# Half-group loads of x and a longer look-ahead in an RMSNorm and matmul kernel

## The chip, the cores and the metric

One core of a Trainium2 chip runs the kernel. The metric is the device time of one execution in microseconds (us). The time of a kernel is the median of repeated runs; a profile comes from one further execution, whose own time stands beside it. In the profile, PE is TensorE (PEld its weight loads), ACT is ScalarE, DVE is VectorE, POOL is GpSimd, and SP is the engine that issues nearly all transfers. Transfers run on 16 DMA engines.

## The reference

Every row of x is divided by its root mean square, scaled by gamma, and multiplied by a weight matrix. x has 16 x 1024 rows of 512 floats (33.6 MB), the output has 768 floats for each row (50.3 MB).

```python
batch, seq, dim, out_dim = 16, 1024, 512, 768
rms = np.sqrt(np.mean(x ** 2, axis=-1, keepdims=True) + eps)
x_norm = x / rms * gamma
return np.matmul(x_norm, weight).astype(np.float32)
```

## The kernel before

The 16,384 rows are cut into 128 tiles of 128 rows, and eight tiles make a group (G = 8), so there are 16 groups. A group of x is one SBUF tile `xt` of 128 partitions x 8 x 512 floats; each partition holds eight rows that lie one after the other in memory, so a whole group is one stretch of 16 KB for each partition, and a group of the output one of 24 KB. Groups 2 to 13 are loaded and stored whole, with one transfer each (2 MB in, 3 MB out). The first two and the last two groups are cut into smaller parts by the table `parts` (line 45): 1, 2, 1, 2, 2 tiles, then 4, 4, and at the end 4, 4 and 2, 2, 2, 1, 1. For a tile i, `first[i]` and `size[i]` are the part that it lies in, and `rows` (line 54) is that part's piece of x or of the output.

Per tile: POOL casts x to bf16 for a pair of tiles (`cast`, line 86, into `xb`), ACT squares it with a running sum (line 90, `jk`), takes the root (line 94), and DVE the reciprocal (line 96). PE transposes the bf16 words (line 113, into PSUM `tp`), DVE copies them to SBUF (line 120, `xT`), and PE multiplies with the weights in four steps of 512 and 256 columns (line 147, PSUM `ops`). ACT finishes the even tiles and DVE the odd ones: they scale the product with the reciprocal into the output tile `ot` (lines 130 and 132). `store` (line 144) sends a part when its last tile is done.

The order of all instructions is written by hand. In the main loop, pair j computes tiles 2j and 2j+1; at its head it issues the loads that `load_until(2*j + AHEAD)` finds due, then the cast of pair j+3 and the norms of pair j+1, and among its matmuls the transposes of a later pair. `load_until` (with `load`, line 75, doing the transfer) walks through the list `starts` and issues each load whose first tile lies below the given bound. Before the loop, three tiles are loaded, then the weights in two halves, then all that starts below AHEAD.

Loads and stores are issued by SP in program order: an instruction that waits holds up all behind it. Each transfer signals one of eight semaphores in rotation, and waits at its issue for the transfer that had the same semaphore before. There are 5 buffers for groups of x, 4 for cast pairs, 3 for groups of the output.

Of the kernel before, what the change touches and what calls it, by code (L numbers as in the profile page):

```python
# [18 lines left out]
def kernel(  # L19
# [8 lines left out]
    nc = tc.nc  # L28
    P = 128

    x = x.flatten_outer_dims()
    out = out.flatten_outer_dims()
# [3 lines left out]
    NT = N // P  # L36
    NP = NT // 2
    G = 8
    NG = NT // G
    AHEAD = 20  # L40
    WIDE = 512

    parts = {0: [1, 2, 1, 2, 2], 1: [4, 4], NG - 2: [4, 4], NG - 1: [2, 2, 2, 1, 1]}
    first, size = {}, {}
    for g in range(NG):
        i = g * G
# [4 lines left out]

    def rows(ap, i):
        return ap[first[i] * P:(first[i] + size[i]) * P, :].rearrange("(p t) d -> p t d", t=size[i])

    singles = ctx.enter_context(tc.tile_pool(name="singles", bufs=1))
    xin = ctx.enter_context(tc.tile_pool(name="xin", bufs=5))
# [8 lines left out]
    x_tiles, xb_tiles, tp_tiles, rstd_of, xT_tiles, o_tiles = {}, {}, {}, {}, {}, {}  # L67

    def held(tiles, i, n=1):
        return tiles[i // G][:, i % G:i % G + n, :]  # L70

    def load(i):
        if i // G not in x_tiles:
            x_tiles[i // G] = xin.tile([P, G, D], F32, name="xt")
        nc.sync.dma_start(out=held(x_tiles, i, size[i]), in_=rows(x, i))

    starts = [i for i in range(NT) if first[i] == i]

    def load_until(i):
        while starts and starts[0] < i:  # L80
            load(starts.pop(0))
# [52 lines left out]
    def accumulator():  # L134
        return opsum.tile([P, 2, WIDE], F32, name="ops").rearrange("p a b -> p (a b)")

# [5 lines left out]
    def store(i):  # L142
        if i == first[i] + size[i] - 1:
            nc.sync.dma_start(out=rows(out, i), in_=held(o_tiles, first[i], size[i]))

    def matmul(i, k, acc, lo, hi):
        nc.tensor.matmul(out=acc[:, lo:hi], lhsT=xT_tiles[i // 2][:, i % 2, k // 2, :, k % 2], rhs=w_bf[:, k, lo:hi],  # L147
                         start=(k == 0), stop=(k == K - 1))


    def matmuls(i, acc, ks, feed=None):
        for k in ks:
            matmul(i, k, acc, 0, WIDE)
            if feed:
                feed()
            matmul(i, k, acc, WIDE, O)

# [19 lines left out]
    with tc.manual_schedule():  # L177
# [9 lines left out]
        for h in range(2):  # L187
            nc.sync.dma_start(out=w_f32[:, 2 * h:2 * h + 2, :].rearrange("p c o -> p (c o)"), in_=wv[:, h, :])
        load_until(AHEAD)


        warm = singles.tile([P, WIDE], BF16)
        nc.vector.memset(warm, 0.0)  # L193
# [6 lines left out]
        def warm_up(n):  # L200
            for _ in range(n):
                nc.tensor.matmul(out=spare[:, :WIDE], lhsT=warm[:, :P], rhs=warm, start=True, stop=True)  # L202

        w_bf = singles.tile([P, K, O], BF16)

        def weights(k, engine, lo=0, hi=O):
            scale(engine, w_bf[:, k, lo:hi], w_f32[:, k, lo:hi], g_sb[:, k % 2, k // 2:k // 2 + 1])
# [21 lines left out]
        acc = [accumulator() for _ in range(4)]  # L229
        weights(0, nc.vector, 0, WIDE)  # L230
        weights(0, nc.vector, WIDE, O)
# [26 lines left out]
        for j in range(2, NP):  # L258
            load_until(2 * j + AHEAD)
            if j + 3 < NP:  # L260
# [61 lines left out]
```

## Time and profile before

| | us |
|---|---|
| median of 10 runs | 211.41 |
| lowest and highest of them | 211.07, 211.89 |
| the profiled execution | 211.58 |
| its span, first to last instruction | 209.8 |
| PE busy | 201.2 |
| ACT busy | 158.2 |
| DVE busy | 111.8 |
| POOL busy | 66.2 |

The span is what the profile covers; 1.8 us of the profiled execution's time lie around it. A busy time is the sum of an engine's instructions. Transfers have two times of their own: that of their issue on SP, and that from issue to landing, when the last of the 16 DMA engines has signalled. Typical ones of before, in us from issue to landing: 16.0 for a whole group's store (3 MB), 20.5 for a whole group's load (2 MB), 13.8 for a load of 1 MB, 8.9 for a store of 384 KB. The core reads 35.13 MB and writes 50.33 MB, 407 GB/s over the span.

### The profile page before, as it was taken

The numbers are of one execution on the slowest core, as the hardware profiler recorded it, in microseconds if no ns is written. First come the engines' busy times: TensorE is split into PE (matmuls) and PEld (weight loads), VectorE is DVE, ScalarE is ACT, GpSimd is POOL, SyncE is SP. The second block draws the span as 40 slices with busy tenths as digits, with TensorE's granted clock in tenths as the row PEclk, the third lists the DMA queues.
The fourth block names the chain that finished last, engine by engine and source line by source line (L and its number), as shares of the span: only waits on it lengthen the run. The fifth ranks groups of instructions, "written<-read, shape, count | busy, mean of one in ns | idle before, by whom it ended". The sixth has DMA issues, their size and how long they took to land.

```text
span 209.8 us, 3598 instructions
## 1 busy us (share of the span) xinstructions
PE 201.2 (96%) x1297; PEld 138.0 (66%) x1297; DVE 111.8 (53%) x204; ACT 158.2 (75%) x388; POOL 66.2 (32%) x71
## 2 busy tenths in 40 slices
PE   7999999999999999999999999999999999999960
PEld 2566777666776666776667766667766677666630
DVE  2555654564465456545644654565456446545630
ACT  4589787788778777877887787778778877877830
POOL 2057341607233323323252332324133305050000
PEclk9999999999999999999999999999999999999997
DMA  6999999999999999999999999999999999998983
GB/s 219 412 429 412 390 419 410 429 421 440 444 406 451 414 434 426 423 434 422 440 423 437 417 442 431 415 440 409 444 414 447 405 426 391 424 432 357 412 349 148
DMA packets 8070, 85.69 MB, mean 408 GB/s; under 512 B 1138, under 2 KB 1140, under 8 KB 3956
## 3 DMA queue, kind: packets, MB, share of 16 engines
q1 hardware_dynamic: 7776, 85.46, 97.1%
q8 instruction: 10, 0.16, 0.3%
q10 hardware_dynamic: 276, 0.00, 0.1%
q14 instruction: 8, 0.07, 0.1%
HBM read 35.13 MB, written 50.33 MB: 407 GB/s over the span
## 4 chain that ended last, share of the span: by engine, by line
PE 94%; DVE 1%; ACT 1%; issue 0%
PE ops L147 78%; PE tp L113 13%; PE ops L202 3%; DVE ot L132 1%; ACT ot L130 0%; DVE xT L120 0%; ACT jk L90 0%; PE tp L224 0%; ACT rms L94 0%; DVE warm L193 0%; DVE rstd L96 0%; DVE eps_sb L195 0%
## 5 line engine op out<-in xcount | busy, mean ns | idle before, releaser
L147 PE MATMUL ops<-w_bf,xT 128*128 128x256 bf16 (+1 forms) x1024 | 194.0, 326 | 0.1
L147 PEld LDWEIGHTS <-xT 128*128 128x128 bf16 x1024 | 100.2, 98 | 56.2 <-DVE xT L120 0.9
L86 POOL CAST xb<-xt 128x1024 bf16<-128x1024 f32 (+1 forms) x65 | 65.5, 1016 | 120.6 <-DMA xt<-in_x_dram 66.1
L120 DVE COPY xT<-tp 128x1024 bf16<-128x1024 bf16 (+1 forms) x67 | 44.5, 667 | 81.3 <-PE tp L113 81.3
L130 ACT ACTIVATE ot<-ops,rstd 128x768 f32<-128x768 f32 (+1 forms) x65 | 58.1, 894 | 37.7 <-PE ops L147 36.9
L90 ACT ACTIVATE jk<-xt 128x512 bf16<-128x512 f32 x128 | 78.7, 619 | 1.1 <-DMA xt<-in_x_dram 1.1
L113 PE MATMUL tp<-ident_f,xb 128*128 128x128 f32 x256 | 69.1, 275 | 0.1
L132 DVE TENSOR_SCALAR ot<-ops,rstd 128x768 f32<-128x768 f32 (+1 forms) x65 | 64.5, 992 | 2.9 <-PE ops L147 2.8
L113 PEld LDWEIGHTS tp<-ident_f,xb 128*128 128x128 f32 x256 | 36.0, 142 | 4.8 <-issue 1.0
L90 ACT ACTIVATION_READ_ACCUMULATOR jk<-xt 128x1 f32 x128 | 24.4, 190 | 0.0
L94 ACT ACTIVATE rms<-ssq,eps_sb 128x2 f32<-128x2 f32 (+1 forms) x64 | 18.9, 295 | 2.0
L96 DVE RECIPROCAL rstd<-rms 128x2 f32<-128x2 f32 (+1 forms) x64 | 10.0, 156 | 3.3 <-ACT rms L94 3.2
L202 PE MATMUL ops<-warm 128*128 128x512 bf16 x15 | 5.7, 531 | 1.2 <-DVE eps_sb L195 1.2
L202 PEld LDWEIGHTS <-warm 128*128 128x128 bf16 x15 | 1.7, 124 | 3.1 <-issue 1.4
L130 ACT ACTIVATE w_bf<-w_f,g_sb 128x768 bf16<-128x768 f32 x2 | 1.9, 935 | 2.4 <-DMA w_f<-in_weight_dram 2.4
L184 ACT ACT_TABLE_LOAD x1 | 1.3, 1283 | 1.8 <-issue 1.8
L86 DVE CAST xb<-xt 128x512 bf16<-128x512 f32 x2 | 1.1, 557 | 2.3 <-DMA xt<-in_x_dram 2.3
L132 DVE TENSOR_SCALAR w_bf<-w_f,g_sb 128x512 bf16<-128x512 f32 (+2 forms) x3 | 1.4, 485 | 0.9 <-DMA w_f<-in_weight_dram 0.9
L193 DVE MEMSET warm<- 128x256 uint32 x1 | 0.3, 272 | 0.9 <-PEq L303 0.9
L224 PE MATMUL tp<-ident_f,g_row 2*128 2x2 f32 x2 | 0.4, 264 | 0.3 <-DVE xT L120 0.3
L224 PEld LDWEIGHTS tp<-ident_f,g_row 2*128 2x128 f32 x2 | 0.3, 201 | 0.5 <-DVE xT L120 0.5
masks.py:199 POOL TENSOR_SCALAR_AFFINE_SELECT ident_f<-ident_f 128x128 f32<-128x128 f32 x1 | 0.3, 294 | 0.1
(7 smaller groups left out, 0.8 us busy)
## 6 DMA issues: line engine op xcount, KB each, us to landing
out_dram<-ot SPq DMA_DIRECT2D x12, 3072.0 KB, 16.0
xt<-in_x_dram SPq DMA_DIRECT2D x12, 2048.0 KB, 20.5
out_dram<-ot SPq DMA_DIRECT2D x4, 1536.0 KB, 11.5
out_dram<-ot SPq DMA_DIRECT2D x6, 768.0 KB, 9.1
xt<-in_x_dram SPq DMA_DIRECT2D x4, 1024.0 KB, 13.8
xt<-in_x_dram SPq DMA_DIRECT2D x6, 512.0 KB, 14.3
w_f<-in_weight_dram SPq DMA_DIRECT2D x2, 768.0 KB, 6.9
out_dram<-ot SPq DMA_DIRECT2D x4, 384.0 KB, 8.9
```

Of the source, the lines that this page charges most:

```text
L86: engine.tensor_copy(out=xb_tiles[i // 2][:, i % 2:i % 2 + n, :], in_=held(x_tiles, i, n))
L90: nc.scalar.activation(out=jk, in_=held(x_tiles, i)[:, 0, :], func=AF.Square, accum_out=ssq)
L94: nc.scalar.activation(out=rms[:, :n], in_=ssq[:, :n], func=AF.Sqrt, scale=1.0 / D, bias=eps_sb)
L96: nc.vector.reciprocal(out=rstd[:, :n], in_=rms[:, :n])
L113: nc.tensor.transpose(out=tp_tiles[j][:, t, h, :], in_=words[:, lo:lo + P], identity=ident_f)
L120: nc.vector.tensor_copy(out=dst[:, t:t + n, :], in_=src[:, t:t + n, :])
L130: nc.scalar.mul(out=dst, in_=src, mul=r)
L132: nc.vector.tensor_single_scalar(out=dst, in_=src, scalar=r, op=mybir.AluOpType.mult)
L147: nc.tensor.matmul(out=acc[:, lo:hi], lhsT=xT_tiles[i // 2][:, i % 2, k // 2, :, k % 2], rhs=w_bf[:, k, lo:hi], start=(k == 0), stop=(k == ...
L184: nc.scalar.preload_act_table(AF.Sqrt)
L202: nc.tensor.matmul(out=spare[:, :WIDE], lhsT=warm[:, :P], rhs=warm, start=True, stop=True)
L224: nc.tensor.transpose(out=gp[:, c, :], in_=g_row[:, :, c], identity=ident_f[:2, :2])
```

## The change

The look-ahead goes from 20 to 24 tiles, and no load has more than four tiles: a whole group comes in two loads, each of 8 KB for each partition, from the same rows of memory as before (so a partition's two pieces of 8 KB lie one behind the other, and the pieces of one load have a pitch of 16 KB). Both halves still go into one SBUF tile `xt`. Parts of four tiles and fewer are loaded as before, apart from the look-ahead. The stores are not touched.

```diff
-    AHEAD = 20
+    AHEAD = 24
...
+    HALF = 4
...
     def load(i):
         if i // G not in x_tiles:
             x_tiles[i // G] = xin.tile([P, G, D], F32, name="xt")
-        nc.sync.dma_start(out=held(x_tiles, i, size[i]), in_=rows(x, i))
-
-    starts = [i for i in range(NT) if first[i] == i]
+        n = min(size[i], HALF)
+        t = i - first[i]
+        nc.sync.dma_start(out=held(x_tiles, i, n), in_=rows(x, i)[:, t:t + n, :])
+
+    starts = [i for i in range(NT) if (i - first[i]) % HALF == 0]
```

## The prediction

> **What bounds the kernel now.** I read the page's busy rows first, then its queue row, then the busy time by stretches, the timeline of the SP queue, SP's waits, and the time from issue to landing of single transfers.
>
> ```profile
> PE 201.2 (96%) x1297; PEld 138.0 (66%) x1297; DVE 111.8 (53%) x204; ACT 158.2 (75%) x388; POOL 66.2 (32%) x71
> PE   7999999999999999999999999999999999999960
> DMA  6999999999999999999999999999999999998983
> q1 hardware_dynamic: 7776, 85.46, 97.1%
> ```
>
> Two resources are full at once: TensorE, and the 16 DMA engines, all fed through SP's one queue. By stretches (after the engines' columns: granted clock, DMA share, GB/s):
>
> ```profile
> 72.00:84.00 12.00, 12.00 (x81) 8.40 (x79) 6.75 (x12) 9.52 (x25) 4.17 (x4) 1.00 1.01 431
> 132.00:144.00 12.00, 12.00 (x81) 8.39 (x80) 6.61 (x13) 9.64 (x24) 4.17 (x4) 1.00 1.00 427
> 205.00:206.00 1.00, 0.00 (x0) 0.00 (x0) 0.00 (x0) 0.00 (x0) 0.00 (x0) 1.00 1.00 402
> 206.00:207.00 1.00, 0.00 (x0) 0.00 (x0) 0.00 (x0) 0.00 (x0) 0.00 (x0) 1.00 0.32 126
> 207.00:208.00 1.00, 0.00 (x0) 0.00 (x0) 0.00 (x0) 0.00 (x0) 0.00 (x0) 0.80 0.14 55
> 208.00:209.00 1.00, 0.00 (x0) 0.00 (x0) 0.00 (x0) 0.00 (x0) 0.00 (x0) 0.50 0.03 12
> ```
>
> In the middle PE has no idle time. Its work by the chain comes in steps of 0.759 us, 1.518 us a tile; 128 tiles make 194.3 us, and 8.57 us (first real matmul) + 194.3 = 202.9, which is where the last matmul ends. So an earlier x can't speed PE. But the span goes on to 209.8: all engines are through by 203.5, and for 206 to 209 only a few DMA engines still work (share 0.32, 0.14, 0.03). That tail is the second bound. The SP queue and two of its transfers' times:
>
> ```profile
> 59.32 0.33 SPq L144 DMA_DIRECT2D out_dram<-ot  x1
> 59.74 0.39 SPq L75 DMA_DIRECT2D xt<-in_x_dram  x1
> 71.46 0.33 SPq L144 DMA_DIRECT2D out_dram<-ot  x1
> 71.89 0.44 SPq L75 DMA_DIRECT2D xt<-in_x_dram  x1
> ```
>
> ```profile
> SPq L144 <- DVE ot L132: 166.6, 24, 11.3
> ```
>
> ```profile
> out_dram<-ot SPq DMA_DIRECT2D x1, 3072.0 KB, 15.4
> xt<-in_x_dram SPq DMA_DIRECT2D x1, 2048.0 KB, 19.8
> out_dram<-ot SPq DMA_DIRECT2D x1, 384.0 KB, 5.5
> ```
>
> The transfers are the store issued at 47.17, the load at 47.59 and the last store at 203.50. SP waits 166.6 us, all at stores (L144): a load behind a store leaves 0.4 us after it, whatever AHEAD says, as long as no store stands between. And a 3 MB store takes 15.4 us, although its 8 packets per engine of 24 KB (912 ns each by the trace's packet records) are 7.3 us: it queues.
>
> The trace also has the 16 arrivals of every transfer's semaphore, one for each DMA engine. Of the last store, twelve come at 206.47 to 206.64, 3.0 us after its issue, and the others at 206.86, 207.93, 207.97 and 208.96. The last arrival of each of the last six transfers stands at 201.45, 203.38, 205.26, 207.11, 208.05 and 208.96: steps of 1.93, 1.88, 1.85, 0.94, 0.91 us, which is what 8 packets of 6,144 B (234 ns) or 3,072 B (121 ns) and a semaphore packet (9 ns) take. The slowest engine is thus busy without a pause up to the end, 2.5 us behind the quick ones. Its total work sets the time.
>
> **What the Trainium skill says.** "DMA: Bandwidth & Descriptors", section "Queues, rings and completion order": an engine takes descriptors in ring order, so a load put ahead of a store delays it on that ring; the steps above agree. Same page, "Why small descriptors are slow": a fixed cost per packet. The trace has it: median 309 ns for 8,192 B, 611 for 16,384, 912 for 24,576; two of the first are 618, so about 7 ns a packet. Same page, "Latency and other measured facts", HBM row pitch: lock-stepped streams at large power-of-two pitches lose bandwidth (an inference there). No run here shows it for 8 KB rows at a 16 KB pitch.
>
> **The change part by part.**
> 1. *AHEAD.* Before, group g is due at pair j = 4g-9; after, its halves are due at 4g-11 and 4g-9. The store of group m stands at the end of pair 4m+3. Both due times of group m+4 (4m+5 and 4m+7) fall between the stores of groups m and m+1, as the old one did, so in the middle SP issues the same bytes at the same moment. It hides nothing and costs nothing. At the start the loads still reach tile 23 before the loop; tiles 24-27 then move ahead of the store of 4-5, and 32-35 ahead of the store of 8-11: each such store is held up by one half load, 8 x 309 + 9 ns = 2.5 us. Output buffers have room: a 3 MB store is issued 16 tiles (24.3 us) before its buffer is wanted and lands after 16, so 8 us are left. At the end, tiles 116-119 move from behind store 11 to behind store 10, and 122-125 from behind store 12 to behind store 11. Loads end sooner; the bytes are the same, on an engine that never pauses: nothing.
> 2. *Halves.* Groups 2 to 13, twelve of them, are split. Per group each engine has 16 packets of 309 instead of 8 of 611, and one more semaphore packet: 16 x 309 - 8 x 611 + 9 = 65 ns. Twelve times: 0.78 us. The first half lands some 2.4 us sooner; but POOL's waits for x (66.1 us) hide behind PE already.
> 3. *SP and its slots.* Twelve more issues of 0.3 to 0.7 us on SP, which waits 166.6 us anyway. Semaphores rotate over eight, so a transfer waits for the eighth before it; with three per group instead of two that is 24 us back or more, against 20 us to land. At the start the load of 20-23 waits for the first weight load (landed at 7.80) and leaves at about 7.8 to 8.2 us, with some 8 us of reads still queued (tiles 12-15 land from 16.5 on). Nothing.
>
> On an engine with slack, 65 ns would vanish: the quick engines' last arrival can move 0.78 us and stay covered by the slow one. On the slowest engine each ns is passed to the end. So the profiled execution (span 209.8, whole 211.58) becomes 212.36, and the median 211.41 becomes **212.2**.
>
> The unknown is how fast half rows are read. Nearest row: the 8 KB loads of tiles 8-15, contiguous, mean 313 ns over 512 such packets. The 16 KB packets have a mean of 626, since 67 of 1,536 took over 60 ns too long; 18.6 us of such excess, over 16 engines, falls before 47 us. With means on both sides the split costs 12 x (16 x 313.3 - 8 x 625.8 + 9) ns = 0.18 us; with none of the 16 KB excess kept it can gain; with the excess doubled it loses more. I take the medians, since the excess belongs to a stretch of time rather than to every packet.
>
> **The rivals.**
> - *Faster.* The slow long reads go. They fall where the engines run in step, from the first 16 KB load on, and the contiguous 8 KB loads just before had none. On the slowest engine the load of 16-23 took from 17.88 to 24.19, 6.3 us where 4.9 are its packets' sum: 1.4 us lost once, and the lag is 4.2 us by 47. If halves save half of a loss of some 3 us on that engine, 1.5 - 0.8 = 0.7 us are gained: 210.7. It decides from 0.78 us saved on; the end of the quick engines caps the gain at 2.5 us (208.9). Against it: a half row keeps the 16 KB pitch.
> - *Slower by more.* Half rows at that pitch, read in step, meet in fewer places of HBM. If the slow reads double on the slowest engine (another 1 us or so of mean excess, 18.6/16 = 1.2): 212.2 + 1.2 = 213.4.
> - *No change.* The means hold (0.18 us), or the engine that is last changes: 211.5.
>
> **How the numbers follow.** This kernel's runs tell 0.2% (0.42 us) from no change. Forecast 0.50, with its own range 211.9 to 212.7; faster rival 0.25; slower by more 0.13; no change 0.12. Slower is 0.50 + 0.13 = 0.63, same 0.12, faster 0.25. The range: down to 210.4, which leaves out about a third of the faster case, and up to 213.6, which leaves out a third of the slow one; some 0.13 outside.
>
> **What would show it.** SP's order in the middle: a store, then two loads. The last matmul still near 202.9. Loads of 1 MB, packets of 8,192 B at about 309 ns, and the last arrival of the last store near 209.7, its quick engines near 206.5. I'm wrong if the slow packets before 47 us are gone or many more, if the last engine's arrivals at the end are no longer in steps of its packets' sums, or if PE shows a wait.

## The result, and the profile after

The changed kernel takes 212.77 us (median of 9 runs, 212.48 to 212.94), the kernel before in the same session 211.39. The ratio is 1.0063, 95% interval 1.0051 to 1.0074: it is slower by 1.33 us, 1.1 to 1.6. The profiled execution took 212.48 us, and its span went from 209.8 to 210.7.

The page after, busy time, the DMA row and the queue:

```profile
PE 201.5 (96%) x1297; PEld 138.1 (66%) x1297; DVE 111.7 (53%) x204; ACT 158.2 (75%) x388; POOL 66.6 (32%) x71
DMA  6999999999999999999999999999999999998992
q1 hardware_dynamic: 9504, 85.46, 96.8%
```

The same bytes (85.46 MB) come in 9,504 packets instead of 7,776: 12 groups x 16 engines x (8 more packets and one for the semaphore) = 1,728. No engine's busy time has moved by more than 0.4 us. The stretches in the middle and at the end (last three columns: granted clock, DMA share, GB/s):

```profile
72.00:84.00 12.00, 12.00 (x81) 8.44 (x80) 6.75 (x12) 9.62 (x24) 4.17 (x4) 1.00 1.01 427
132.00:144.00 12.00, 12.00 (x81) 8.44 (x80) 6.60 (x13) 9.52 (x25) 4.15 (x4) 1.00 1.01 426
206.00:207.00 1.00, 0.00 (x0) 0.00 (x0) 0.00 (x0) 0.00 (x0) 0.00 (x0) 1.00 0.46 178
207.00:208.00 1.00, 0.00 (x0) 0.00 (x0) 0.00 (x0) 0.00 (x0) 0.00 (x0) 1.00 0.07 28
208.00:209.00 1.00, 0.00 (x0) 0.00 (x0) 0.00 (x0) 0.00 (x0) 0.00 (x0) 0.58 0.06 25
209.00:210.00 1.00, 0.00 (x0) 0.00 (x0) 0.00 (x0) 0.00 (x0) 0.00 (x0) 0.50 0.01 3
```

PE is as full as before in the middle. At the end a share of 0.06 is one of 16 engines: a single DMA engine works on alone from 207 to beyond 209, where before the last bytes came before 209. The SP queue, from the same place as before:

```profile
59.53 0.34 SPq L149 DMA_DIRECT2D out_dram<-ot  x1
59.97 0.86 SPq L80 DMA_DIRECT2D xt<-in_x_dram  x2
71.68 0.34 SPq L149 DMA_DIRECT2D out_dram<-ot  x1
72.12 0.86 SPq L80 DMA_DIRECT2D xt<-in_x_dram  x2
```

A store, then both halves, 0.44 us after it: the longer look-ahead does not bring the bytes of the middle any sooner. Who waits for x has changed all the same. Before, and then after (in total us, times, longest):

```profile
POOL xb L86 <- DMA xt<-in_x_dram: 66.1, 19, 7.5
POOL xb L86 <- PE tp L113: 49.9, 31, 2.0
```

```profile
POOL xb L91 <- PE tp L118: 105.1, 54, 2.0
POOL xb L91 <- DMA xt<-in_x_dram: 11.8, 4, 4.0
```

POOL's waits for loads fall by 54 us and its waits for PE rise by 55, and the kernel gets nothing for it: this is idle time of an engine that isn't the bottleneck. Both parts of the change have a share in it: in the experiments below, each with one profile, the waits for loads are 41.9 us with the longer look-ahead alone and 30.8 with the halves alone.

The semaphore records of the last six transfers tell where the span grew. The last of each transfer's 16 arrivals came, before, at 201.45, 203.38, 205.26, 207.11, 208.05, 208.96; after, at 202.10, 204.03, 205.88, 207.73, 208.65, 209.57. The steps are the same to 0.03 us (1.93, 1.85, 1.85, 0.92, 0.92 us after): over these transfers the slowest engine doesn't pause in either kernel, and it is later by 0.61 us. From the last arrival to the end of the span there are 0.83 us before and 1.09 after. 0.61 + 0.26 = 0.87 us, the growth of the span. The second term is a surprise; the SP waits at the program's end show it. Before, and then after:

```profile
SPq L317 <- DMA out_dram<-ot: 4.9, 4, 1.8
```

```profile
SPq L322 <- DMA out_dram<-ot: 5.5, 1, 5.5
```

Before, SP waits four times for a store; after, once, and for the whole time. The end of the program waits for the eight DMA semaphores in five steps of a fixed order, of two semaphores each (two of the ten aren't DMA semaphores), and a step that finds its semaphores already there still takes some 0.065 us. Before, the last transfer's semaphore stands in the fifth step, which ends at 209.01, just behind the arrival at 208.96. After, it stands in the first: that one ends at 209.62, behind the arrival at 209.57, and the other four at 209.69, 209.75, 209.82 and 209.88. Four times 0.065 us is the 0.26. In which step the last semaphore stands follows from the number of transfers modulo eight.

### The profile page after: what moved, and what is told of

Read it like the earlier page. It is cut to its first block, busy times and chain, and to the rows that moved or that the text cites. A ratio compares the mean times of both kernels' runs of the same rounds, so it can differ in the third digit from the quotient of the medians.

```text
span 210.7 us, 3610 instructions
## 1 busy us (share of the span) xinstructions
PE 201.5 (96%) x1297; PEld 138.1 (66%) x1297; DVE 111.7 (53%) x204; ACT 158.2 (75%) x388; POOL 66.6 (32%) x71
## 3 DMA queue, kind: packets, MB, share of 16 engines
q1 hardware_dynamic: 9504, 85.46, 96.8%
## 4 chain that ended last, share of the span: by engine, by line
PE 93%; DMA 1%; DVE 1%; ACT 1%; issue 0%
PE ops L152 78%; PE tp L118 13%; DMA xt<-in_x_dram 1%; PE ops L207 1%; DVE ot L137 1%; ACT ot L135 0%; DVE xT L125 0%; ACT jk L95 0%; DVE xb L91 0%; PE tp L229 0%; ACT rms L99 0%; DVE rstd L101 0%
```

## The experiments

All ratios are against the kernel before on the same chip, with 95% intervals; us over before are the ratio less one, times 211.5. All the edits are to the kernel before unless told otherwise.

### Taking the change apart

```diff
-        nc.sync.dma_start(out=held(x_tiles, i, size[i]), in_=rows(x, i))
+        n = min(size[i], 4)
+        for t in range(0, size[i], n):
+            nc.sync.dma_start(out=held(x_tiles, i + t, n), in_=rows(x, i)[:, t:t + n, :])
```

> Halves alone: every whole group in two loads issued one right after the other, where the one load stood, look-ahead 20. Theory (the slowest DMA engine pays a fixed cost for every packet and sets the end): 65 ns x 12 groups = 0.78 us over before, ratio 1.0037. Rival (the look-ahead, which puts loads ahead of stores, is what costs): no more than the packets' cost here, and clearly less than the changed kernel's 1.0063. Rival (half rows are read slower than whole ones): about 1.006, all of the changed kernel's loss.

Measured: 1.0052 (1.0034 to 1.0070), 1.1 us. The last arrival came at 209.73, 0.77 us later than before, and 1.10 us of the span lay behind it (0.83 before). The look-ahead by itself:

```diff
-    AHEAD = 20
+    AHEAD = 24
```

> Look-ahead alone: 24 tiles, whole loads. Theory: same bytes and packets on an engine that never pauses, 0 +- 0.2 us, ratio 1.000. Rival (order): +0.5 us or more, ratio 1.0025.

Measured: 1.0013 (0.9998 to 1.0028), no change that can be told. So the halves carry the loss; up to some 0.6 us from the look-ahead can't be excluded. Its one profile had its last arrival at 209.41, with no more behind it than before (0.83).

The changed kernel, run again in another session:

> The changed kernel once more, beside the two others on the same chip: 1.0063 within 0.0015, and a profile of its own, whose slowest DMA engine should again be busy in steps of its packets up to the end; the last arrival and the span move together.

Measured: 1.0059 (1.0043 to 1.0074); last arrival 209.69, steps of 1.91, 1.85, 1.85, 0.93, 0.90 us before it, 1.10 us behind it. In this profile the last matmul ended at 202.70, in the first one at 203.14, against 202.92 before: PE's end has nothing to do with the loss.

### Does the slowest DMA engine set the end?

```diff
+        spare_x = singles.tile([P, 2, D], F32)
...
+            if j == 31:
+                nc.sync.dma_start(out=spare_x, in_=rows(x, 4))
```

> The kernel before with one more load of 512 KB in the middle of the loop into a buffer that nothing reads: it adds eight packets of 4 KB and a semaphore packet to each DMA engine. Theory: 8 x 159 + 9 ns = 1.28 us are passed to the end in full, ratio 1.0061. Rival (the end follows PE, or engines have slack that takes this up): 0, ratio 1.000.

Measured: 1.0060 (1.0040 to 1.0080), 1.27 us. A load that no instruction reads, issued at 96.8 us, more than 110 us ahead of the end, costs its full price there (forecast 1.28; the interval is 0.8 to 1.7, and 0.11 of it are waits at the end, as below). Its last second of transfers:

```profile
208.00:209.00 1.00, 0.00 (x0) 0.00 (x0) 0.00 (x0) 0.00 (x0) 0.00 (x0) 0.50 0.13 52
209.00:210.00 1.00, 0.00 (x0) 0.00 (x0) 0.00 (x0) 0.00 (x0) 0.00 (x0) 0.50 0.06 25
```

Two engines (0.13) and then one (0.06) are left. The first arrival of the last store is at 206.66, against 206.47 before: on the quick engines nearly all of the extra work was swallowed. On the slowest the last arrival is 1.44 us later. That the end follows the slowest engine's work is shown.

### Is it the packets, or the transfers?

The same 8 KB packets, but in one transfer: a gap in the SBUF tile cuts each partition's 16 KB in two (the readers of the tile follow it).

```diff
...
-            x_tiles[i // G] = xin.tile([P, G, D], F32, name="xt")
+            x_tiles[i // G] = xin.tile([P, G // CUT, CUT * D + 16], F32, name="xt")
+        if size[i] == G:
+            nc.sync.dma_start(out=x_tiles[i // G][:, :, :CUT * D], in_=rows(x, i).rearrange("p (c t) d -> p c (t d)", t=CUT))
+            return
```

> One load for each group as before, but its SBUF tile has a gap of 64 bytes between the two halves of a partition, so each engine has 16 packets of 8 KB for it, the two halves of a row one after the other. Same number of transfers as before. Theory: 12 x 8 x 7 ns = 0.67 us over before, ratio 1.0032, packets of 309 ns. Rival (what costs is the second transfer, or the halves' pitch of 16 KB): no loss, 1.000, or clearly less than halves alone.

Measured with CUT = 4: 1.0010 (0.9997 to 1.0022), 0.2 us, and a last arrival at 208.96, as before. It had all the packets,

```profile
q1 hardware_dynamic: 9312, 85.46, 97.6%
xt<-in_x_dram SPq DMA_DIRECT2D x12, 2048.0 KB, 20.2
```

1,536 more than before in the same number of transfers, each with a median record of 309 ns. The interval ends at 0.47 us, so my theory's 0.67 isn't there: by the kernel's time, two pieces of one row in one transfer cost hardly more than the row, though the records' sum says otherwise. With CUT = 2, pieces of 4 KB:

> One load for each group with a gap of 64 bytes after every two tiles: 32 packets of 4 KB for each engine where there were 8 of 16 KB, still one transfer. Theory A (about 7 ns for each packet, one after the other): 32 x 159 - 8 x 611 = 200 ns x 12 groups = 2.4 us over before, ratio 1.0114. Theory B (packets of one transfer overlap; it is a further transfer that costs): at most 0.4 us, ratio 1.002 or less.

Measured: 1.0069 (1.0055 to 1.0084), 1.46 us. Neither theory: 24 more packets for each group and engine cost 1.46 us / 12 / 24 = 5 ns each, not the 8 that the records' difference gives, and more than theory B allows. Then transfers without work:

```diff
+    spare_x = singles.tile([16, 2, 128], F32)
...
+        if size[i] == G and i > 2 * G:
+            for t in range(2):
+                nc.sync.dma_start(out=spare_x[:, t:t + 1, :], in_=rows(x, i)[:16, t:t + 1, :128])
```

> The kernel before with two tiny loads behind each load of groups 3 to 13, 22 in all, of 16 partitions x 512 bytes into a buffer that nothing reads: one packet of 512 bytes and a semaphore packet for each engine. Theory A (sum of the packets, some 26 + 9 ns each): 0.77 us, ratio 1.0036. Theory B (a transfer has a cost of its own of some 80 ns on every engine): 22 x 0.08 to 0.1 = 1.8 to 2.2 us, ratio 1.0085 to 1.0104.

Measured: 1.0045 (1.0026 to 1.0064), 0.95 us, some 0.13 of which is the end's waits (0.96 us behind the last arrival). What is left agrees with the sum of packets, 0.77, and not with 80 ns for each transfer. SP itself waits 71.9 us at these loads, since they share one buffer, but the DMA engines stay full (share 1.00 and 1.02 in the stretches from 60 to 84 us). A transfer as such is cheap.

### Is it the pitch of 16 KB?

Three loads instead of two, at the place of the one:

```diff
-        nc.sync.dma_start(out=held(x_tiles, i, size[i]), in_=rows(x, i))
+        for t, n in {8: [(0, 3), (3, 3), (6, 2)]}.get(size[i], [(0, size[i])]):
+            nc.sync.dma_start(out=held(x_tiles, i + t, n), in_=rows(x, i)[:, t:t + n, :])
```

> Every whole group in three loads of 3, 3 and 2 tiles, issued one after the other where the one load stood, look-ahead 20. Theory A: 8 x (234 + 234 + 159) - 8 x 611 + 2 x 9 = 146 ns x 12 = 1.75 us, ratio 1.0083. Theory B: two further transfers for each group cost twice what one costs in halves alone (1.1 us): 2.2 us, ratio 1.0104. A cost of reading half rows at a 16 KB pitch that is paid once: about 1.1 us, as with halves alone.

Measured: 1.0173 (1.0154 to 1.0192), 3.7 us, more than any of the theories. All engines are behind here, not one:

```profile
206.00:207.00 1.00, 0.00 (x0) 0.00 (x0) 0.00 (x0) 0.00 (x0) 0.00 (x0) 0.50 1.00 418
209.00:210.00 1.00, 0.00 (x0) 0.00 (x0) 0.00 (x0) 0.00 (x0) 0.00 (x0) 0.50 1.02 415
```

The 6 KB packets between 47 and 144 us have a mean of 262 ns with a median of 234; the slowest hundredth took 864 and more. The same numbers of tiles, but each piece read from rows that lie one behind the other:

```diff
...
+            src = x[(i + t) * P:(i + t + n) * P, :].rearrange("(p t) d -> p t d", t=n)
+            nc.sync.dma_start(out=held(x_tiles, i + t, n), in_=src)
```

> Three loads of 3, 3 and 2 tiles, each read from rows one behind the other (6, 6 and 4 KB), again with rows of x at other places in their group, so the output is in another order there. If the pitch of 16 KB made three loads cost 1.0173: no more than the packets' sum, 1.75 us, ratio 1.004 to 1.008. If not: 1.017 again.

Measured: 1.0072 (1.0056 to 1.0087), 1.5 us: near the packets' sum of 1.75 us. The mean of the 6 KB packets between 47 and 144 us is now 239 ns. So pieces of 6, 6 and 4 KB at a pitch of 16 KB pay 2 us for the way in which they lie in memory. For halves the same edit with pieces of 4 and 4 tiles:

> Halves alone as before (two loads of four tiles where the one stood), but each half is read from 8 KB rows that lie one behind the other (pitch 8 KB, not 16 KB). So x's rows come to other places in their group, and the output is another than the reference's by the order of rows in groups 2 to 13; work, packets and stores are the same. If the pitch of 16 KB is what halves alone pay for (1.0052): 0.2 to 0.7 us over before, ratio 1.001 to 1.003. If it is the boundary between two transfers, or the packets: the same 1.005 as halves alone.

Measured: 1.0062 (1.0045 to 1.0080), the same as with the pitch of 16 KB (1.0052 to 1.0063). For halves the pitch is not the cause.

### The end's waits

No kernel was made for them, but fourteen profiles give the time from the last arrival to the end of the span, and their numbers of transfers differ:

| kernels | transfers | modulo 8 | behind the last arrival, us |
|---|---|---|---|
| before, look-ahead alone, the two cut ones | 56 | 0 | 0.83 each |
| three loads, both | 80 | 0 | 0.83 each |
| one extra load; merged loads and stores | 57; 49 | 1 | 0.94; 0.94 |
| merged loads | 51 | 3 | 1.07 |
| changed kernel (two profiles), halves alone, halves near | 68 | 4 | 1.09, 1.10, 1.10, 1.10 |
| tiny loads | 78 | 6 | 0.96 |

Kernels with the same remainder agree within 0.01 us, whatever they do before. In the traces with remainder 1 and 6 the last semaphore stands in the third step, with 3 and 4 in the first, with 0 in the fifth.

### Two tries at a faster one

If the slowest engine's work is what counts, fewer and larger transfers should help. First the last two groups' loads whole and the last stores in 8, 4, 2, 1, 1 tiles:

```diff
-    parts = {0: [1, 2, 1, 2, 2], 1: [4, 4], NG - 2: [4, 4], NG - 1: [2, 2, 2, 1, 1]}
+    parts = {0: [1, 2, 1, 2, 2], 1: [4, 4], NG - 1: [4, 2, 1, 1]}
...
+        n = size[i] if i < NT - 2 * G else G
+        nc.sync.dma_start(out=held(x_tiles, i, n), in_=rows(x, i, n))
...
```

> The other way round: the last two groups are loaded whole (two transfers for seven) and the last stores merged into 8, 4, 2, 1, 1 tiles (five for seven and more bytes in each packet). Theory (the slowest DMA engine's sum of work sets the end): by the packets' times 0.37 us less for the loads and 0.13 us for the stores, by a cost of some 80 ns for each of seven transfers saved 0.56 us; 0.4 to 0.9 us faster than before, ratio 0.996 to 0.998. Rival (the last stores' latency sets the end): later stores make it 1 us slower or more.

Measured: 1.0039 (1.0024 to 1.0053), slower, as the rival said, by 0.8 us. The stretches of this kernel, then of the one before:

```profile
185.00:190.00 5.00, 5.00 (x35) 3.50 (x33) 3.37 (x6) 3.85 (x11) 1.04 (x1) 1.00 0.79 339
190.00:193.00 3.00, 3.00 (x22) 2.09 (x21) 1.69 (x3) 2.42 (x6) 0.00 (x0) 1.00 0.14 55
193.00:200.00 7.00, 7.00 (x47) 4.62 (x46) 3.37 (x6) 5.73 (x13) 0.00 (x0) 1.00 0.93 394
```

```profile
185.00:190.00 5.00, 5.00 (x36) 3.49 (x34) 3.37 (x6) 3.92 (x11) 1.89 (x2) 1.00 0.99 421
190.00:193.00 3.00, 3.00 (x22) 2.10 (x20) 1.69 (x3) 2.42 (x6) 0.00 (x0) 1.00 0.94 397
193.00:200.00 7.00, 7.00 (x47) 4.67 (x45) 3.38 (x6) 5.74 (x13) 0.00 (x0) 1.00 0.88 363
```

Waiting for eight tiles leaves the engines idle for 3 us (share 0.14 instead of 0.94), and all of them, the quick ones too, then have the 3 MB store to do at the end: the first arrival of the last store is at 208.96, not 206.47. Then only the loads of the last two groups merged, the stores in their old sizes:

> Only the loads of the last two groups merged (two for nine), the stores as before but from rows at a pitch of 24 KB. Theory (sum of the slowest engine's work): 0.37 us less by the packets' times, ratio 0.998, if the merged loads don't delay the stores behind them. Rival (a 2 MB load late in the queue stands in front of a store that the quick engines then have to do at the end): same or slower, as with the merged stores (1.0039).

Measured: 1.0005 (0.9988 to 1.0022), no change. In its profile the last arrival was 0.18 us sooner, and the end's waits were 0.24 us longer. No version here beats the kernel before.

## Why the prediction came out as it did

- **What bounds the kernel.** Right, and shown by the extra load: PE's end stays within 202.7 to 203.3 in all kernels but the three loads at 16 KB (203.75), and the span follows the last DMA engine.
- **AHEAD, nothing.** Right within what can be told (1.0013, interval over 1.0000). In the middle the loads leave SP where they did.
- **Halves, 0.78 us.** The size holds for the last arrival: +0.61 and +0.73 us in the two profiles of the changed kernel, +0.77 with halves alone. That it fits is luck in good part, for the loss didn't come in twelve steps of 65 ns. The last arrival of the store of group 6 came at 111.6 to 112.1 us in the four profiles whose loads are whole and in the old order up to there (before: 111.80), but at 110.28 and 110.55 in the changed kernel, and at 111.10 with halves alone. Up to there the slowest engine was 0.7 to 1.5 us ahead of the kernel before, where the sum for eight split groups says 0.52 behind; from there to the end it lost 1.5 to 2.1 us, where the sum for four groups says 0.26. Why it loses so much so late was not settled. The reason as I put it (each packet pays its 7 ns, wherever it stands) fails elsewhere too: in one transfer the same packets cost 0.2 us instead of 0.67, and 4 KB packets 1.46 instead of 2.4. The prediction's own steps at the end had a sign of this: 8 packets of 121 ns and one of 9 are 0.977 us, and the steps were 0.94 and 0.91. The sum of records fits the totals, within their intervals, where the pieces are transfers of their own (halves, three loads from near rows, tiny loads), and is too high inside one transfer. Why two pieces of a row are cheap only in one transfer was not settled. For halves the pitch is out, and so is a charge of 80 ns for each transfer.
- **SP and its slots, "Nothing".** This step failed. I counted the issues and the waits for a slot, and left out the end, where SP waits for the eight slots in turn. Twelve more transfers shift the last one by four places, and four waits, 0.26 us, come behind the last arrival instead of ahead.
- **The sum.** 0.78 + 0.26 = 1.04 us, against 1.33 (1.1 to 1.6) measured, 1.25 (0.9 to 1.6) in the second session and 0.87 in the first pair of profiles. Some 0.3 us of the first is not attributed; a part of it may be the look-ahead, whose interval reaches 0.6 us (in its one profile the last arrival is 0.45 us later than before). So the time came in the stated range, on the forecast side, and just above the likeliest case's own 211.9 to 212.7.
- **The faster rival.** Its premise seemed to come true, and with it, in part, one of my signs of being wrong (slow packets before 47 us that are gone): from 17 to 47 us the large loads' packets had a total excess over their median of 18.6 us in the kernel before, and 7.8 us in the changed one (10.2 in the second profile), and at 45 us the slowest engine was 2.3 us behind the quickest, not 4.2. But half rows are not what did it. By the same count, halves alone have 17.6 us of excess and the halves from near rows 15.6, the look-ahead alone 16.2, and four more kernels with whole loads in the old order 11.4 to 15.3. Only the two profiles with both parts of the change lie lower; why is not known. And it brought nothing, since at the store of group 11 one engine was 5.3 us behind in the changed kernel (4.9 before). From 107 us on its distance grows by 0.35 to 0.4 us with each group, once by 1.1; before, it went from 4.6 to 5.2 and back to 4.9. The trace has fetches of instructions among its DMA packets: in both kernels one of 16 KB, for about 1 us, every 18 to 20 us in this stretch, and several times a store's packet shortly behind one took some 0.4 us longer than its kind's median. They come at the same times in both and not with each group, so they don't explain the difference, and the trace doesn't name the engine of a packet. The cause stays open.
- **Slower by more.** Not for halves; it happened with three loads.

The Trainium skill ("Perfetto Trace Analysis", section "DMA Optimizations") says that splitting transfers can help where DMA engines are generally idle. This case fits: the engines have a share of 1.01 in the middle, the split makes the kernel 1.1 us slower by itself, and POOL's 54 us less of waiting is worth nothing.

## What to carry to other kernels

Where the engines are through and transfers still run, look at each transfer's 16 arrivals: if the last one's steps are near its packets' sums, the slowest DMA engine is the bound, and a load put on it is paid at the end, here even from 110 us ahead. Price a split by what stands on that engine, not by how much sooner some other engine gets its data; and measure that price, since the records' sum was three times too high in one of these kernels and half of what was paid in another. And merging at the end has its own price: a store that waits for more tiles left the engines idle for 3 us first and busy last.

## What the runs showed of the hardware that was not expected

- The order of the final semaphore waits is worth up to 0.27 us, set by the number of transfers modulo eight (0.83 to 1.10 us behind the last arrival).
- A row of 16 KB cut into two packets in one transfer costs about 0.2 us (0 to 0.5) over 96 rows on each engine; cut into four, 1.46 us. As two transfers it costs 1.1 us, some 0.27 of which are the waits at the end.
- Pieces of 6, 6 and 4 KB at a pitch of 16 KB cost 3.7 us, the same pieces from near rows 1.5 us; for 8 KB halves the pitch makes no difference that can be told (1.1 and 1.3 us).
